# Five of eight row pairs of two matrix products by Strassen's algorithm, in an encoder kernel on one core

## The chip, the cores and the metric

The kernel runs on one core of one Trainium2 chip. The metric is the device time of one execution in microseconds; a lower time is better. The engines are TensorE (PE, with its weight loads PEld), VectorE (DVE), ScalarE (ACT), GpSimd (POOL) and SyncE (SP), which here only issues loads. SBUF is the memory that the engines compute from, PSUM the eight banks of 128 x 512 float32 that TensorE writes its sums to.

## What is computed

Two layers of an encoder on 256 tokens of width 2048, in float32. Cut to what matters:

```python
for l in range(DEPTH):                       # 2 layers
    u = rmsnorm(x, norm_mix[l])
    proj = u @ w_in[l]                       # 2048 x 8256: queries, keys, values, two gates
    ...                                      # y_a: latent attention @ w_o_mla, y_b: neighbourhood attention @ w_o_na
    merged = jax.nn.sigmoid(gate_a) * y_a + jax.nn.sigmoid(gate_b) * y_b
    x = x + merged @ w_out[l]                # 2048 x 2048
    h = rmsnorm(x, norm_mlp[l]) @ w_ff1[l]   # 2048 x 8192
    x = x + jnp.square(jax.nn.relu(h)) @ w_ff2[l]   # 8192 x 2048
return rmsnorm(x, norm_final)
```

## The kernel before

All products run on TensorE in a rounded float32 format. To keep float32 accuracy each operand is split in two: `hi`, the rounded value (a copy on ACT), and `lo`, the rest (a subtraction on DVE, `lo = raw - hi`, both inputs in SBUF). A product of two split operands takes three matmuls, hi x hi, hi x lo and lo x hi, summed in one PSUM bank.

Weights stream from memory through `weights` (L157): a load of 1 MB by SP into one of three `raw` buffers, ACT's cast to `hi` (L172) and DVE's subtraction to `lo` (L173), both on 128 x 1024 elements, into four `hi` and four `lo` buffers. There are two forms of product:

- `gemm_a` (L215) has the activations stationary (128 tokens by 128 rows) and 512 weight columns moving; its result has tokens on the partitions. It holds two banks, one per 128 tokens, and runs over 16 row blocks, two at a time: 96 matmuls for 512 columns. It serves w_out, w_ff2, the gates and the attention output products.
- `gemm_b` (L227) has the weights stationary and 256 tokens moving, hi and lo side by side in a 512-wide matmul, then a 256-wide one; its result is transposed, ready to be the next product's activation. It serves w_in's attention parts and w_ff1.

The MLP runs in four blocks of 2048 hidden columns. A block is four `gemm_b` of 512 hidden columns (w_ff1), whose results `relu2` (L639) adds up, squares and splits into `pair` tiles (hi and lo of 256 tokens), and four `gemm_a` (w_ff2), whose results `residual` (L612) adds to x (`xt`, L617 and L619), scaled there by the square of the row norm. In w_out, `turned` (L319) transposes the merged attention output on TensorE into the activations, column group by column group as the group is finished.

The order of the instructions comes from the program text and from a list scheduler at build time, which may move an instruction of an engine ahead of others; each engine then executes its own list strictly in order, with waits on the others. Small attention steps are slipped between matmuls by `tick`. PSUM is used as five banks under the tag `bank` and three under `abank` (`ABANKS`). POOL does little: the mask sum of the neighbourhood attention (L416), sums of squares (L275), a power of the norms (L259) and a few small loads.

Of the kernel before, what the change touches and what calls it, by code (L numbers as in the profile page):

```python
# [26 lines left out]
F32 = mybir.dt.float32  # L28
F32R = mybir.dt.float32r
# [26 lines left out]
NSLOT, ABANKS, SMALL, RBUFS, HBUFS = 44, 3, 8, 3, 4  # L56
# [6 lines left out]
def trunk(ctx: ExitStack, tc: tile.TileContext, x, w_in, w_uq, w_ukv, rpb, w_o_mla, w_o_na,  # L63
# [3 lines left out]
    wpool = ctx.enter_context(tc.tile_pool(name="wpool", bufs=4))  # L67
    slots = ctx.enter_context(tc.tile_pool(name="slots", bufs=NSLOT))
    tmp = ctx.enter_context(tc.tile_pool(name="tmp", bufs=2))
    psum = ctx.enter_context(tc.tile_pool(name="psum", bufs=8, space=bass.MemoryType.PSUM))  # L70

    def bank():
# [12 lines left out]
    def small():  # L85
        return tmp.tile([P, S], F32, tag="small", name="small", bufs=SMALL)
# [70 lines left out]
    def weights(w, nk, c0, n, before=None):  # L157
# [3 lines left out]
        for k0 in range(0, nk, 2):  # L161
# [6 lines left out]
            hi = wpool.tile([P, 1024], F32R, tag="hi", name="hi", bufs=HBUFS)  # L168
            lo = wpool.tile([P, 1024], F32R, tag="lo", name="lo", bufs=HBUFS)
# [6 lines left out]
    def weights_twice(w, nk, c0, n):  # L176
# [4 lines left out]
        for k0 in range(0, nk, 8):  # L181
            hi = wpool.tile([P, 1024], F32R, tag="hi", name="hi", bufs=HBUFS)
            lo = wpool.tile([P, 1024], F32R, tag="lo", name="lo", bufs=HBUFS)
# [58 lines left out]
    def rows_of(col):  # L242

        dg = [tmp.tile([P, P], F32, tag="diag", name="diag", bufs=4) for _ in range(2)]
# [6 lines left out]
        row = tmp.tile([P, S], F32, tag="rrow", name="rrow", bufs=4)  # L251
# [3 lines left out]
    def root(v, width, name):  # L255

        nc.vector.tensor_scalar(v, v, 1.0 / width, EPS, op0=ALU.mult, op1=ALU.add)  # L257
        col = tmp.tile([P, 2], F32, tag="rcol", name=name, bufs=6)
        nc.gpsimd.tensor_tensor(col, v, mhalf, op=ALU.pow)  # L259
        return col  # L260

    class Norm:
# [14 lines left out]
        def scales(self):  # L277
# [5 lines left out]
            v = tmp.tile([P, 2], F32, tag="var", name="var", bufs=2)  # L283
# [4 lines left out]
    class RowNorm:  # L288


        def __init__(self):
            self.sums = tmp.tile([P, 2, 4], F32, tag="sums", name="sums", bufs=2)

        def add(self, t, c4):
            junk = tmp.tile([P, 512], F32, tag="junk", name="junk", bufs=1)
# [3 lines left out]
        def scale(self):  # L299
            v = tmp.tile([P, 2], F32, tag="var", name="var", bufs=2)  # L300
# [3 lines left out]
        def scales(self):  # L304

            self.scale()
            self.half = tmp.tile([P, 2], F32, tag="rcol", name="half", bufs=6)
# [3 lines left out]
        def square(self):  # L311

            self.scale()
            self.sq = tmp.tile([P, 2], F32, tag="rcol", name="sq", bufs=6)
            nc.vector.tensor_tensor(self.sq, self.col, self.col, op=ALU.mult)
            return
            yield
# [157 lines left out]
    for l in range(DEPTH):  # L475
        wi = w_in[l]
# [116 lines left out]
        mg = [None] * NC  # L593
        for c4 in range(4):
            th = [None] * 2

            def merge(t, ps):
# [3 lines left out]
                if t == 1:  # L601
                    start(turned(lambda t, c4=c4: part[t, c4], c4, mg, lambda c: 0.5), 2)
# [4 lines left out]
            gemm_a(w_o_mla[l], c4 * 512, att, merge)  # L607


        last = l == DEPTH - 1  # L610

        def residual(c4, scale=None, n=None, then=None):  # L612

            def evac(t, ps):
                cs = xt[t][:, c4 * 512:(c4 + 1) * 512]
                if scale is None:
                    nc.vector.tensor_tensor(cs, cs, ps, op=ALU.add)  # L617
                else:
                    nc.vector.scalar_tensor_tensor(cs, ps, scale.sq[:, t:t + 1], cs, op0=ALU.mult, op1=ALU.add)  # L619
                if n is not None:  # L620
                    n.add(t, c4)
                if then is not None and t == 1:
                    start(then(c4), 2)
            return evac
# [3 lines left out]
        for c4 in range(4):  # L628
            gemm_a(w_out[l], c4 * 512, mg,
# [101 lines left out]
```

## Time and profile before

| | before |
|---|---|
| median of three runs, us | 2689.84 (2689.79 to 2690.21) |
| the profiled execution, us | 2689.91 |
| its span in the profile, us | 2688.1 |
| TensorE busy, us | 2666.8 (99%) |
| DVE busy, us | 1602.9 (60%) |
| ACT busy, us | 1277.1 (48%) |
| POOL busy, us | 60.5 (2%) |
| memory traffic, mean | 185 GB/s |

The span runs from the first to the last instruction that the profile records. A group of instructions is one line of the program on one engine with one shape; it has a count, its busy time, the mean duration of one in ns, and the idle time of its engine just before, with what ended that idle time. Matmuls overlap in the pipeline, so their durations add up to more than the time they take; the distance from one start to the next is what a matmul costs.

### The profile page before, as it was taken

What the parts mean: (1) busy time and instruction counts of PE and PEld (TensorE: products, weight loads), DVE (VectorE), ACT (ScalarE), POOL (GpSimd) and SP (SyncE); (2) the same over time, 40 slices, a digit from 0 to 9 for tenths busy, and PEclk for the clock granted to TensorE, in tenths of its full rate; (3) what the DMA queues carried; (4) which work ended last, traced back from release to release, by engine and by line L of the source; (5) the groups of instructions that cost most, each with busy time, mean ns of one, the idle gap of its engine ahead of it and who ended that gap; (6) DMA issues with size and microseconds to landing.
All of it is one profiled execution on the core that took longest, in us unless ns stands there. A gap on an engine that the chain in (4) does not pass through costs nothing.

```text
span 2688.1 us, 34037 instructions
## 1 busy us (share of the span) xinstructions
PE 2666.8 (99%) x13596; PEld 2268.7 (84%) x13596; DVE 1602.9 (60%) x2158; ACT 1277.1 (48%) x1815; POOL 60.5 (2%) x86
## 2 busy tenths in 40 slices
PE   8999999999999999999999999999999999999998
PEld 7888888888888888888888888888888888888886
DVE  5676486555655546556567754955556555565554
ACT  5554465444434434444445544644444344443443
POOL 1110000000000000000001100000000000000000
PEclk9999999999999999999999999999999999999999
DMA  7555644555565555555555555455555555655554
GB/s 231 184 165 189 195 161 155 189 184 180 186 203 186 190 190 186 197 193 189 183 183 179 171 187 183 153 167 188 188 188 188 189 187 194 208 189 193 188 188 141
DMA packets 253839, 496.49 MB, mean 185 GB/s; under 512 B 12688, under 2 KB 16784, under 8 KB 253680
## 3 DMA queue, kind: packets, MB, share of 16 engines
q1 hardware_dynamic: 250624, 488.14, 55.2%
q0 software_dynamic: 2048, 4.56, 0.6%
q8 instruction: 106, 1.74, 0.3%
q10 hardware_dynamic: 1008, 1.61, 0.2%
q14 instruction: 53, 0.43, 0.0%
HBM read 492.18 MB, written 2.10 MB: 184 GB/s over the span
## 4 chain that ended last, share of the span: by engine, by line
PE 84%; issue 14%; DVE 1%; DMA 1%; ACT 0%; POOL 0%; SPq 0%; POOLq 0%; DVEq 0%; ACTq 0%
PE bank L194 21%; PE bank L199 16%; PE bank L200 16%; PE bank L201 16%; PE bank L195 11%; DMA raw<-in_w_in 1%; PE abank L206 1%; PE abank L205 1%; PE abank L204 1%; PE abank L326 1%; PE abank L377 0%; DVE lo L173 0%; DVE wide L670 0%; PE abank L347 0%; ACT hi L172 0%
## 5 line engine op out<-in xcount | busy, mean ns | idle before, releaser
L173 DVE TENSOR_TENSOR lo<-raw,hi 128x1024 fp32r<-128x1024 f32 (+1 forms) x928 | 1132.5, 1222 | 977.8 <-ACT hi L172 973.0
L172 ACT CAST hi<-raw 128x1024 fp32r<-128x1024 f32 (+1 forms) x928 | 971.8, 1049 | 1131.1 <-PE bank L201 736.2
L194 PE MATMUL bank<-pair,hi 128*128 128x512 f32 x3008 | 1059.0, 398 | 2.3 <-DVE small L212 1.0
L200 PE MATMUL bank<-lo,pair 128*128 128x512 f32 (+1 forms) x2240 | 866.1, 387 | 0.0
L199 PE MATMUL bank<-hi,pair 128*128 128x512 f32 (+1 forms) x2240 | 865.8, 388 | 0.0
L201 PE MATMUL bank<-hi,pair 128*128 128x512 f32 (+1 forms) x2240 | 865.8, 387 | 0.0
L195 PE MATMUL bank<-pair,lo 128*128 128x256 f32 x3008 | 835.5, 280 | 0.4 <-DVE lo L173 0.3
L194 PEld LDWEIGHTS bank<-pair,hi 128*128 128x128 f32 x3008 | 563.5, 188 | 133.0 <-ACT hi L172 1.9
L195 PEld LDWEIGHTS bank<-pair,lo 128*128 128x128 f32 x3008 | 567.7, 189 | 5.9 <-DVE lo L173 1.6
L201 PEld LDWEIGHTS bank<-hi,pair 128*128 128x128 f32 x2240 | 420.8, 188 | 84.6
L199 PEld LDWEIGHTS bank<-hi,pair 128*128 128x128 f32 x2240 | 420.8, 188 | 84.1
L200 PEld LDWEIGHTS bank<-lo,pair 128*128 128x128 f32 x2240 | 420.9, 188 | 82.6
L150 ACT ACTIVATE pair<-small 128x256 fp32r<-128x256 f32 x200 | 73.6, 413 | 89.8 <-DVE small L641 67.1
L210 ACT COPY small<-bank 128x256 f32<-128x256 f32 x218 | 78.6, 369 | 29.0 <-PE bank L195 27.8
L152 DVE TENSOR_TENSOR pair<-small,pair 128x256 fp32r<-128x256 f32 x200 | 76.6, 418 | 19.2 <-ACT pair L150 19.2
L212 DVE TENSOR_TENSOR small<-bank,small 128x256 f32<-128x256 f32 x218 | 83.0, 416 | 0.2
L259 POOL TENSOR_TENSOR col<-var,mhalf 128x2 f32<-128x2 f32 x9 | 6.3, 702 | 1928.8 <-DVE var L257 1928.8
L619 DVE SCALAR_TENSOR_TENSOR xt<-bank,sq,xt 128x512 f32<-128x512 f32 x64 | 45.0, 744 | 7.8 <-PE bank L201 7.8
L641 DVE SCALAR_TENSOR_TENSOR small<-small 128x256 f32<-128x256 f32 x128 | 48.2, 418 | 0.0
L154 DVE SCALAR_TENSOR_TENSOR pair<-abank,g_sb,pair 128x256 fp32r<-128x256 f32 x64 | 29.2, 478 | 23.0 <-ACT pair L150 23.0
L150 ACT ACTIVATE pair<-abank,g_sb 128x256 fp32r<-128x256 f32 x64 | 28.2, 469 | 27.3 <-PE abank L326 23.4
L150 ACT ACTIVATE pair<-abank 128x256 fp32r<-128x256 f32 x64 | 23.6, 381 | 29.2 <-PE abank L206 19.1
(96 smaller groups left out, 789.9 us busy)
## 6 DMA issues: line engine op xcount, KB each, us to landing
raw<-in_w_ff SPq DMA_DIRECT2D x256, 1024.0 KB, 5.0
raw<-in_w_in SPq DMA_DIRECT2D x124, 1024.0 KB, 5.1
raw<-in_w_out SPq DMA_DIRECT2D x32, 1024.0 KB, 4.9
raw<-in_w_o_na SPq DMA_DIRECT2D x16, 1024.0 KB, 4.9
raw<-in_w_o_mla SPq DMA_DIRECT2D x16, 1024.0 KB, 4.9
raw<-in_w_ukv SPq DMA_DIRECT2D x8, 1024.0 KB, 4.9
raw<-in_w_uq SPq DMA_DIRECT2D x8, 768.0 KB, 4.6
raw<-in_w_in SPq DMA_DIRECT2D x10, 512.0 KB, 4.9
```

Source lines behind the costliest of these rows:

```text
L150: nc.scalar.activation(dst[:, :S], src, AF.Copy, scale=scale)
L152: nc.vector.tensor_tensor(dst[:, S:], src, dst[:, :S].bitcast(F32), op=ALU.subtract)
L172: nc.scalar.copy(hi, src)
L173: nc.vector.tensor_tensor(lo, src, hi.bitcast(F32), op=ALU.subtract)
L194: nc.tensor.matmul(ps, wh, a, start=first, stop=False)
L195: nc.tensor.matmul(ps[:, :S], wl, a[:, :S], start=False, stop=last)
L199: nc.tensor.matmul(ps, a[:, t * P:(t + 1) * P], wh, start=first, stop=False)
L200: nc.tensor.matmul(ps, a[:, t * P:(t + 1) * P], wl, start=False, stop=False)
L201: nc.tensor.matmul(ps, a[:, S + t * P:S + (t + 1) * P], wh, start=False, stop=last)
L210: nc.scalar.copy(h, ps[:, S:])
L212: nc.vector.tensor_tensor(t, ps[:, :S], h, op=ALU.add)
L641: nc.vector.scalar_tensor_tensor(t, t, 0.0, t, op0=ALU.max, op1=ALU.mult)
```

## The change

Rows of the weights are taken in pairs of 128 (`j`, eight pairs for 2048 rows), and columns in halves of 1024. For such a pair the product of a 2 x 2 block matrix of activations (two token halves by two row blocks) with a 2 x 2 block matrix of weights (two row blocks by two halves of 512 columns) needs eight block products, 24 matmuls. For the five pairs in `SPAIRS` the changed kernel forms it with seven block products (Winograd's form of Strassen's algorithm), 21 matmuls, from sums of blocks; the other three pairs run plainly and accumulate into the same banks. This is `gemm_s`, used for w_out and w_ff2; a call covers 1024 columns and holds all eight banks.

The sums of weight blocks are `t13` (POOL, 128 x 1024, two at once) and `t24` (its first half on POOL, its second on DVE). They, `b21` and the two diagonal blocks are split by ACT and DVE as the weights were. The sums of activation blocks (`s1` to `s4`) are made by POOL in `operand`, four instructions of 128 x 128, and split with the blocks. At the end `residual` makes the four output blocks from eight banks: eight DVE adds, one ACT copy and four POOL adds of 128 x 512.

```diff
-NSLOT, ABANKS, SMALL, RBUFS, HBUFS = 44, 3, 8, 3, 4
+NSLOT, SMALL, RBUFS, HBUFS = 44, 8, 3, 4
+
+SPAIRS = (0, 1, 3, 5, 7)
...
     def bank():
-        return psum.tile([P, 512], F32, tag="bank", name="bank", bufs=8 - ABANKS)
-
-    def abank():
-        return psum.tile([P, 512], F32, tag="abank", name="abank", bufs=ABANKS)
+        return psum.tile([P, 512], F32, tag="bank", name="bank", bufs=8)
+
+    abank = bank
...
+    def operand(f, strassen):
+        a11, a21, a12, a22, s1, s2, s3, s4 = (f[:, i] for i in range(8))
+        if strassen:
+            nc.gpsimd.tensor_tensor(s1, a21, a22, op=ALU.add)
+            nc.gpsimd.tensor_tensor(s2, s1, a11, op=ALU.subtract)
+            nc.gpsimd.tensor_tensor(s4, a12, s2, op=ALU.subtract)
+            nc.gpsimd.tensor_tensor(s3, a21, a11, op=ALU.subtract)
+        hi, lo = [], []
+        for i in range(0, 8 if strassen else 4, 4):
+            src = f[:, i:i + 4].rearrange("p a q -> p (a q)")
+            h, lw = pair(), pair()
+            nc.scalar.copy(h, src)
+            nc.vector.tensor_tensor(lw, src, h.bitcast(F32), op=ALU.subtract)
...
+    def turned_pair(src, c, dst, j):
+        tp = abank()
...
+        f = tmp.tile([P, 8, P], F32, tag="f", name="f", bufs=2)
+        nc.scalar.activation(f[:, :4].rearrange("p a q -> p (a q)"), tp, AF.Copy, scale=0.5)
+        dst[j] = operand(f, j in SPAIRS)
...
+    def gemm_s(w, c0, acts, evac):
...
+        for j in range(n):
+            raw = wpool.tile([P, 2048], F32, tag="raw", name="raw", bufs=RBUFS)
+            nc.sync.dma_start(raw.rearrange("p (k n) -> p k n", n=1024),
+                              w[2 * j * P:(2 * j + 2) * P, c0:c0 + 1024].rearrange("(k p) n -> p k n", p=P))
+            if j not in SPAIRS:
+                for k in range(2):
+                    left, right = half(raw[:, k * 1024:(k + 1) * 1024])
+                    ah, al = have(acts, j)
+                    for i, t, side in ((2, 0, right), (3, 0, left), (4, 1, right), (8, 1, left)):
+                        mm3(i, ah[2 * k + t], al[2 * k + t], *side)
...
+                continue
+            b12, b11, b22, b21 = (raw[:, i:i + 512] for i in range(0, 2048, 512))
+            t13 = wpool.tile([P, 1024], F32, tag="t", name="t13", bufs=4)
+            nc.gpsimd.tensor_tensor(t13.rearrange("p (a n) -> p a n", a=2),
+                                    b12.rearrange("p (a n) -> p a n", a=1).to_broadcast([P, 2, 512]),
+                                    raw[:, 512:1536].rearrange("p (a n) -> p a n", a=2), op=ALU.subtract)
+            t24 = wpool.tile([P, 1024], F32, tag="t", name="t24", bufs=4)
+            nc.gpsimd.tensor_tensor(t24[:, :512], b22, t13[:, :512], op=ALU.subtract)
+            nc.vector.tensor_tensor(t24[:, 512:], b21, t24[:, :512], op=ALU.subtract)
+            w11, w22 = half(raw[:, 512:1536])
+            w21, = half(b21)
+            w1, w3 = half(t13)
+            w2, w4 = half(t24)
+            (a11, _, a12, a22, s1, s2, s3, s4), low = have(acts, j)
+            (l11, _, l12, l22, r1, r2, r3, r4) = low
+            mm3(1, a11, l11, *w11)
+            mm3(2, a12, l12, *w21)
+            tick()
+            mm3(3, s4, r4, *w22)
+            mm3(5, s1, r1, *w1)
+            tick()
+            mm3(7, s3, r3, *w3)
+            mm3(6, s2, r2, *w2)
+            tick()
+            mm3(4, a22, l22, *w4)
+        evac(b)
...
+        half_a = ExitStack()
+        wpool = half_a.enter_context(tc.tile_pool(name="wpool", bufs=4, reuse_waits="tile"))
+        tmp = half_a.enter_context(tc.tile_pool(name="tmp", bufs=2, reuse_waits="tile"))
...
-                if t == 1:
-                    start(turned(lambda t, c4=c4: part[t, c4], c4, mg, lambda c: 0.5), 2)
...
+        drain()
+        half_a.close()
...
+        half_b = ExitStack()
+        hbufs, smalls = 5, 3
...
+        for c4 in range(4):
+            for c in range(2):
+                start(turned_pair(lambda t, c4=c4: part[t, c4], c, mg, 2 * c4 + c), 0)
...
+                nc.scalar.copy(p1, b[1])
+                nc.vector.tensor_tensor(x11, x11, b[2], op=ALU.add)
+                nc.gpsimd.tensor_tensor(x11, x11, p1, op=ALU.add)
+                nc.vector.tensor_tensor(x12, x12, b[3], op=ALU.add)
+                nc.vector.tensor_tensor(x22, x22, b[8], op=ALU.add)
+                nc.vector.tensor_tensor(x22, x22, b[5], op=ALU.add)
+                nc.vector.tensor_tensor(u2, p1, b[6], op=ALU.add)
+                nc.vector.tensor_tensor(u4, u2, b[5], op=ALU.add)
+                nc.vector.tensor_tensor(u3, u2, b[7], op=ALU.add)
+                nc.gpsimd.tensor_tensor(x12, x12, u4, op=ALU.add)
+                nc.vector.tensor_tensor(x21, x21, b[4], op=ALU.add)
+                nc.gpsimd.tensor_tensor(x22, x22, u3, op=ALU.add)
+                nc.gpsimd.tensor_tensor(x21, x21, u3, op=ALU.add)
```

The squared row norm is no longer multiplied in `residual`; instead `relu2` multiplies by the row norm before it squares. The weight and scratch pools (`wpool`, `tmp`) are opened anew for each half of a layer, one for the attention (four `hi` and `lo` buffers) and one for w_out and the MLP (five, and four `t` buffers).

How the scheduler places this is shown at three places. The first is DVE in a w_ff2 product. Before, in the first block of layer 0, behind the last `relu2`, splits of the weights alternate with the residual adds of a column group (`xt`, the two token halves):

```order
L641 SCALAR_TENSOR_TENSOR small<-small 128x256
L152 TENSOR_TENSOR pair<-small,pair 128x256
L173 TENSOR_TENSOR lo<-raw,hi 128x1024 x7
L619 SCALAR_TENSOR_TENSOR xt_91<-bank,sq,xt_91 128x512
L619 SCALAR_TENSOR_TENSOR xt_92<-bank,sq,xt_92 128x512
L173 TENSOR_TENSOR lo<-raw,hi 128x1024 x8
```

In the changed kernel, at the end of the first half of that product (`t13_6953` and `t24_6955` are the sums of the last pair, `t13_7014` and `t24_7016` those of the next half's first):

```order
L374 TENSOR_TENSOR lo_6963<-raw_6951,hi_6962 128x512
L374 TENSOR_TENSOR lo_6967<-t13_6953,hi_6966 128x1024
L397 TENSOR_TENSOR t24_7016<-raw_7012,t24_7016 128x512
L374 TENSOR_TENSOR lo_6971<-t24_6955,hi_6970 128x1024
L730 TENSOR_TENSOR xt1_89<-xt1_89,bank_6775 128x512
L727 TENSOR_TENSOR xt0_88<-xt0_88,bank_6692 128x512
L374 TENSOR_TENSOR lo_7020<-raw_7012,hi_7019 128x1024
L729 TENSOR_TENSOR xt0_88<-xt0_88,bank_6696 128x512
L374 TENSOR_TENSOR lo_7024<-raw_7012,hi_7023 128x512
L397 TENSOR_TENSOR t24_7067<-raw_7063,t24_7067 128x512
L731 TENSOR_TENSOR xt1_89<-xt1_89,bank_6700 128x512
L374 TENSOR_TENSOR lo_7028<-t13_7014,hi_7027 128x1024
```

The splits of the next half's first pair stand between the residual adds of the half that ends, and each pair has five DVE instructions in place of two.

The second place is POOL over the same stretch. Before, its list goes from the norms of the attention (L275 sums, L259 powers) straight to the loads of the next layer's attention bias:

```order
L259 TENSOR_TENSOR col<-var,mhalf 128x2
L275 TENSOR_TENSOR acc<-acc,small 128x256 x3
L259 TENSOR_TENSOR col<-var,mhalf 128x2 x3
L412 DMA mb<-in_rpb 64x6x64 x4
L416 TENSOR_TENSOR mb<-mb,mask_sb 128x384 x2
```

In the changed kernel, from the last hidden pair of the block on:

```order
L326 TENSOR_TENSOR f_6640<-f_6640 128x128
L392 TENSOR_TENSOR t13_6875<-raw_6873 128x1024
L396 TENSOR_TENSOR t24_6877<-raw_6873,t13_6875 128x512
L392 TENSOR_TENSOR t13_6953<-raw_6951 128x1024
L396 TENSOR_TENSOR t24_6955<-raw_6951,t13_6953 128x512
L392 TENSOR_TENSOR t13_7014<-raw_7012 128x1024
L396 TENSOR_TENSOR t24_7016<-raw_7012,t13_7014 128x512
L392 TENSOR_TENSOR t13_7065<-raw_7063 128x1024
L396 TENSOR_TENSOR t24_7067<-raw_7063,t13_7065 128x512
L728 TENSOR_TENSOR xt0_88<-xt0_88,u_6995 128x512
L392 TENSOR_TENSOR t13_7144<-raw_7142 128x1024
```

POOL now has two subtractions for each Strassen pair, and its residual adds stand in the same list.

The third place is DVE at the end of a block's w_ff1. Before, the results of the last column group (L212 add, L641 square, L152 split) come between the splits of two weight loads of w_ff2:

```order
L212 TENSOR_TENSOR small<-bank,small 128x256 x3
L641 SCALAR_TENSOR_TENSOR small<-small 128x256 x3
L173 TENSOR_TENSOR lo<-raw,hi 128x1024
L212 TENSOR_TENSOR small<-bank,small 128x256
L152 TENSOR_TENSOR pair<-small,pair 128x256 x3
```

In the changed kernel `small` and `rrow` (the row norm) belong to the last four `relu2`, the `lo` and `t24` to the first two pairs of w_ff2:

```order
L374 TENSOR_TENSOR lo_6673<-raw_6665,hi_6672 128x1024
L397 TENSOR_TENSOR t24_6720<-raw_6716,t24_6720 128x512
L374 TENSOR_TENSOR lo_6677<-raw_6665,hi_6676 128x512
L374 TENSOR_TENSOR lo_6681<-t13_6667,hi_6680 128x1024
L374 TENSOR_TENSOR lo_6685<-t24_6669,hi_6684 128x1024
L770 TENSOR_TENSOR small_6626<-bank_6451,small_6624 128x256
L771 SCALAR_TENSOR_TENSOR small_6626<-small_6626,rrow_5971 128x256
```

All splits of the first pair (`raw_6665`) and the subtraction of the second (`t24_6720`) stand ahead of the last `relu2`, which is where w_ff1's last matmuls end.

More of the change, by code (lines that the diff above doesn't have):

```diff
@@ L242, in rows_of @@
     def rows_of(col):
-        dg = [tmp.tile([P, P], F32, tag="diag", name="diag", bufs=4) for _ in range(2)]
+        dg = [keep.tile([P, P], F32, tag="diag", name="diag", bufs=4) for _ in range(2)]
         for t in range(2):
@@ L627, in trunk, with scaled_mlp @@
         xg = [None] * NC
-        for c4 in range(4):
-            gemm_a(w_out[l], c4 * 512, mg,
-                   residual(c4, None, mlp, lambda c4, xg=xg: turned_x(c4, xg, G_MLP + l * NC)))
-        start(mlp.square(), 10)
+        for g in range(2):
+            gemm_s(w_out[l], g * 1024, mg,
+                   residual(g, mlp, lambda c4, xg=xg: turned_x(c4, xg, G_MLP + l * NC)))
+        def scaled_mlp():
+            start(mlp.scales(), 0)
+            while not hasattr(mlp, "row"):
+                advance(len(pending) - 1)
         norm = RowNorm()
```

130 lines of the change are left out of this document (84 added, 46 removed).

## The prediction

> **What bounds it now.** I read the page's busy shares and chain first, then the stretch in which the change sits, then its groups, and last the few places where POOL computes.
>
> ```profile
> span 2688.1 us, 34037 instructions
> PE 2666.8 (99%) x13596; PEld 2268.7 (84%) x13596; DVE 1602.9 (60%) x2158; ACT 1277.1 (48%) x1815; POOL 60.5 (2%) x86
> PE 84%; issue 14%; DVE 1%; DMA 1%; ACT 0%; POOL 0%; SPq 0%; POOLq 0%; DVEq 0%; ACTq 0%
> ```
>
> TensorE is busy in 2666.8 of 2688.1 us and carries the chain; 21 us are all that other engines cost it. The profiled execution took 2689.91 us, 1.8 beyond its span and within 0.1 of the median 2689.84. I add to 2689.9. A difference under 0.2% (5 us) I count as no change.
>
> The next fence has the busy time by stretch for one w_ff2 product of a block and the w_ff1 products behind it (columns: us, then PE, PEld, DVE, ACT, POOL busy and count, granted clock, DMA share, GB/s).
>
> ```profile
> 729.20:816.30 87.10, 87.10 (x386) 72.18 (x385) 46.98 (x50) 35.29 (x38) 0.00 (x0) 1.00 0.57 191
> 816.30:905.90 89.60, 89.60 (x513) 78.00 (x512) 52.57 (x72) 42.56 (x60) 0.00 (x0) 1.00 0.57 189
> ```
>
> The first stretch is four column groups of 96 matmuls. TensorE has no gap, so one matmul of 512 columns costs 87.10/384 = 0.2268 us. POOL does nothing there, and DVE is idle for nearly half.
>
> **What is removed.** A pair of row blocks takes 24 matmuls plainly and 21 by Strassen. There are 20 products of 1024 columns (2 layers, 1 in w_out and 4 in w_ff2, 2 halves), each with five such pairs: 20 x 5 x 3 = 300 matmuls, 300 x 0.2268 = 68.0 us. One product of 1024 columns goes from 192 x 0.2268 = 43.5 to 177 x 0.2268 = 40.1 us of TensorE; a Strassen pair is 4.76 us of it.
>
> **What is added: operands for DVE and POOL.** A plain pair needs two splits of 1024. A Strassen pair needs three of 1024, one of 512 and a subtraction of 512 on DVE, and subtractions of 1024 (t13) and 512 (t24) on POOL. The groups that price them:
>
> ```profile
> L173 DVE TENSOR_TENSOR lo<-raw,hi 128x1024 fp32r<-128x1024 f32 x32 | 39.2, 1225 | 39.6 <-ACT hi L172 39.4
> L172 ACT CAST hi<-raw 128x1024 fp32r<-128x1024 f32 x33 | 34.8, 1055 | 50.0 <-PE bank L201 49.7 <-PE bank L194 0.2
> L188 DVE TENSOR_TENSOR lo<-raw,hi 128x512 fp32r<-128x512 f32 x8 | 5.2, 689 | 5.3 <-ACT hi L187 5.3
> L187 ACT CAST hi<-raw 128x512 fp32r<-128x512 f32 x8 | 4.6, 618 | 7.8 <-PE bank L194 7.8
> L617 DVE TENSOR_TENSOR xt<-xt,bank 128x512 f32<-128x512 f32 x16 | 10.2, 681 | 0.0
> L641 DVE SCALAR_TENSOR_TENSOR small<-small 128x256 f32<-128x256 f32 x128 | 48.2, 418 | 0.0
> L379 ACT CAST pp<-abank 128x512 fp32r<-128x512 f32 x32 | 18.7, 584 | 17.3 <-PE abank L377 17.1
> ```
>
> DVE per Strassen pair: 3 x 1.225 + 2 x 0.689 = 5.05 us; per plain pair 2.45. ACT per Strassen pair: 3 x 1.055 + 0.618 = 3.8, under TensorE's 4.76, so ACT costs nothing. DVE per product of 1024: 5 x 5.05 + 3 x 2.45 + 8 residual adds of 0.681 = 38.1 us, just under TensorE's 40.1. Were POOL independent, TensorE would stay the bound. Whether it is independent is seen where it computes beside DVE (timeline: start, us, engine and line).
>
> ```profile
> 103.65 1.01 POOL L416 TENSOR_TENSOR mb<-mb,mask_sb 128x384 f32<-128x384 f32 x1 [3.61 <-DMA mb<-in_rpb]
> 192.74 0.74 POOL L275 TENSOR_TENSOR acc<-acc,small 128x256 f32<-128x256 f32 x1 [1.66 <-ACT small L274]
> 108.28 1.01 POOL L416 TENSOR_TENSOR mb<-mb,mask_sb 128x384 f32<-128x384 f32 x1 [2.13 <-DMA mb<-in_rpb]
> 108.46 1.91 DVE L173 TENSOR_TENSOR lo<-raw,hi 128x1024 fp32r<-128x1024 f32 x1
> 182.49 1.22 DVE L173 TENSOR_TENSOR lo<-raw,hi 128x1024 fp32r<-128x1024 f32 x1 [0.42 <-ACT hi L172]
> 182.82 1.76 POOL L416 TENSOR_TENSOR mb<-mb,mask_sb 128x384 f32<-128x384 f32 x1 [2.62 <-DMA mb<-in_rpb]
> 189.91 1.16 POOL L275 TENSOR_TENSOR acc<-acc,small 128x256 f32<-128x256 f32 x1 [5.33 <-ACT small L274]
> 190.39 0.42 DVE L212 TENSOR_TENSOR small<-bank,small 128x256 f32<-128x256 f32 x1
> 214.31 1.23 DVE L173 TENSOR_TENSOR lo<-raw,hi 128x1024 fp32r<-128x1024 f32 x1 [0.22 <-ACT hi L172]
> 215.46 1.36 DVE L154 SCALAR_TENSOR_TENSOR pair<-small,g_sb,pair 128x256 fp32r<-128x256 f32 x2
> ```
>
> At 108.28 POOL runs to 109.29; the split that starts inside it takes 1.91 instead of 1.225, as if begun at 109.14, 0.15 before POOL's end. At 182.49 it is the other way round: POOL takes 1.76 instead of 1.01, as if begun 0.14 before the split's end. So a split (two SBUF inputs) and a POOL instruction exclude each other, with 0.15 us of overlap at a handover. DVE at 190.39, with one input in PSUM, keeps its 0.42 inside a POOL instruction: the residual adds are not excluded. (The Trainium skill, SBUF — State Buffer, section Who interferes with whom, states the exclusion for every VectorE instruction with two SBUF inputs against a GpSimd instruction that reads SBUF; the trace agrees with 1.91 for 1.225, and by that rule the subtractions and operand splits, whose forms no row here shows, are excluded too.)
>
> POOL's clean 0.74 for 256 and 1.01 for 384 elements make 2.11 ns an element and 0.20 us fixed: an estimate of 2.36 us for 1024, 1.28 for 512, 0.47 for 128, reaching 2.7 times beyond the longest row. (The Trainium skill, GPSIMD Engine Reference, section Elementwise — side-by-side cycle accounting, gives 4497 ns for 2048 elements; by its half and quarter, an estimate, the sum below would be some 45 us smaller. The trace's slope is kept.)
>
> Exclusive time of a Strassen pair: 5.05 + 2.36 + 1.28 = 8.69; less four handovers of 0.15, and 0.07 for each of three DVE instructions that follow another DVE instruction (214.31 + 1.23 is 215.54, the next starts at 215.46): 7.9 us, against TensorE's 4.76. Ends: 8.69 without any overlap, 7.5 if every instruction costs only its row less 0.15 and POOL's fixed part vanishes at its borders.
>
> **Sum for one w_ff2 block (two products of 1024 columns), from the last w_ff1 matmul on.** Ten Strassen pairs 79.0; six plain ones 14.7; POOL's four residual adds of the first half 4 x 1.28 = 5.1; the last hidden pairs still to be formed 5.7 (four POOL of 0.47, three DVE of 0.689, four of 0.418). Ready ahead, as the order shows: the first pair 7.9 and the second's POOL part with its DVE subtraction 4.3, so -12.2. The last product after its split: 1.0. The eight DVE residual adds run under POOL's instructions: 0, with 5.4 per product as the other end. Total 93.3 us, against 87.1: +6.2. Behind it w_ff1 waits 1.5 for its first split, queued behind two residual adds of 0.681 (the next five are made while TensorE works on three). Eight blocks: 8 x 7.7 = +62.
>
> **w_out.** Nothing is ready ahead here: the transposed operands start only after the first half's pools close. Added to 79.0 + 14.7 + 5.1 + 1.0: 20 POOL instructions of 0.47 and 13 DVE splits of 0.689 for the operands, 18.4; and a start during which TensorE waits for bank copy 0.584, four POOL 1.9, cast 0.618, cast of the weights 1.055 and a first split, about 5 (0 if the order hides it, 7 with all handovers). 123.2 against 87.1 (the same 384 matmuls before), and 1.5 behind: +37.6, twice +75.
>
> ```profile
> raw<-in_w_ff SPq DMA_DIRECT2D x256, 1024.0 KB, 5.0
> SPq L167 <- DVE lo L173: 1909.6, 369, 9.1
> ```
>
> **Smaller edits.** Loads keep their number and size and wait for buffers (second row), not for the DMA; one per 4.76 us is the fastest demand, with three buffers for 5.0 us of landing: 0. Between the layers the pools change once more, with a load and a split to wait for, and the last residual chain (DVE adds, two POOL adds of 1.28, norm) is longer: 5 each, +10. The per-row scale that moves from the residual to relu2 replaces an operand of an existing instruction: 0, hidden in w_ff1, where DVE is busy for 52.57 of 89.60. One tag for all eight banks: 0, since a half's banks are freed while its last products run; if not, 0.7 per half.
>
> Sum: 62 + 75 + 10 = +147, in which the 68 us of removed matmuls are contained. 2689.9 + 147 = 2837 us.
>
> **Rivals.**
> 1. *POOL is hidden, faster.* POOL's instructions fall where DVE waits for ACT's casts (39.6 us in the stretch above), and TensorE stays the bound: -68 + 2 x 5 + 10 x 1.5 + 10 = -33, 2657 us. For it: DVE alone needs 38.1 of 40.1. Against it: in those waits DVE has no split ready, but the splits then only come later, and exclusive time is 93 in 87. It decides where a Strassen pair's exclusive time is under 7.05 us (with H for it, a block with its wait behind is 9 H + 23.7 by the sum above, and 87.1 at 7.05); full gain below 6.3.
> 2. *Residual not covered.* DVE's order puts residual adds that wait for the last products ahead of the next splits; all 5.4 us per product then count: 20 x 5.4 = +108, 2945 us. For it: DVE executes in order. Against it: most splits of the next pair stand between the adds.
> 3. *The clock falls.* TensorE waits 7.9 - 4.76 = 3.1 us in each of three Strassen pairs in a row (last of one half, first two of the next). At half clock these 14.3 us double, of which the waits absorb 9: +5 to +14 per block, ten blocks, 2887 to 2977.
>
> ```profile
> 0.00:18.00 18.00, 9.71 (x32) 7.16 (x32) 2.59 (x4) 7.43 (x15) 7.34 (x18) 1.00 0.88 258
> ```
>
>    Against it: TensorE busy for only 9.71 of these 18 us, and the granted clock stays 1.00. (The Trainium skill, TensorE: Matmul & The Clock Gate, section Part 1: The HAM clock gate, halves the clock after an idle window of about 3.4 us; by that rule waits of 3.1 would just escape. This row shows no fall.)
>
> **Chances.** My sum 0.58, with its own range 2750 to 2940 (100 Strassen pairs x -0.4, four more instructions ready ahead per block -36 and no start -10, to x +0.8 and a quarter of rival 2's adds); rival 2 0.13; rival 3 0.04; rival 1 0.20; the sum meeting its point of balance, no change, 0.03; 0.02 for a slight gain or loss of other cause. Faster 0.22, same 0.03, slower 0.75. For 8 in 10 the range runs from 2675, inside rival 1, to 2960.
>
> **What would show it.** Right: TensorE busy for about 92% of the span (2666.8 - 68 in 2835) with waits on lo splits in the w_out and w_ff2 stretches; the 1024 splits' mean well over 1225 ns, and POOL's t13 well over 2.36 where they meet; DVE and POOL busy times together near the length of those stretches. Matmuls of 512 columns 300 fewer at 0.2268 either way. Wrong: split means still at 1225 with POOL active, TensorE without gaps in w_ff2, or the POOL instruction of 1024 far from 2.36.

## The result, and the profile after

The changed kernel takes 2912.32 us (median of four runs, 2906.73 to 2917.03), the kernel before 2689.82 (2688.95 to 2690.21) on the same chip. The ratio is 1.0827, 95% interval 1.0807 to 1.0847: slower, by 222.5 us. The forecast was 2837 with a range of 2675 to 2960.

The first two parts of the page after (busy time of each engine; then the span in 40 slices, with the granted clock):

```profile
PE 2715.9 (93%) x13304; PEld 2241.7 (77%) x13304; DVE 2204.2 (76%) x2514; ACT 1499.9 (52%) x2149; POOL 839.6 (29%) x566
...
PE   8999999879989899899889999998899898998996
...
POOL 1110000362352543534401100003524435435244
PEclk9999999899999999999899999999999999999998
```

TensorE is busy for longer than before (2666.8) with 300 fewer matmuls of 512 columns (292 fewer in all; in part because some of them run at half clock, see the last section), and its row shows gaps where POOL's row shows work: the stretches with w_out and the MLP. What TensorE waits for (us in all, times, longest), and then the groups of DVE and POOL in those stretches with different shapes kept apart:

```profile
PE bank L368 <- DVE lo L374: 123.4, 106, 3.8
PE bank L368 <- ACT hi L373: 11.4, 8, 4.8
PE bank L368 <- DVE small L770: 11.0, 8, 1.8
```

```profile
L374 DVE TENSOR_TENSOR lo<-raw,hi 128x1024 fp32r<-128x1024 f32 x220 | 376.0, 1737 | 10.6 <-ACT hi L373 10.0
L374 DVE TENSOR_TENSOR lo<-t,hi 128x1024 fp32r<-128x1024 f32 x200 | 281.4, 1422 | 8.2 <-ACT hi L373 7.8
L333 DVE TENSOR_TENSOR pair<-f,pair 128x512 fp32r<-128x512 f32 x130 | 127.3, 983 | 15.1 <-ACT pair L332 14.8
L397 DVE TENSOR_TENSOR t<-raw,t 128x512 f32<-128x512 f32 x100 | 112.2, 1122 | 90.4 <-POOL t L396 90.4
```

```profile
L392 POOL TENSOR_TENSOR t<-raw x100: 2357/2593/3527, 553.3 to 2882.0; 128x1024 f32<-128x1024 f32 x100
```

Before, TensorE waited 7.4 us for the input and at most 1.0 for any other cause; now 123.4 us for `lo`, and once in each block 1.3 to 1.8 for an add of `relu2` (`small`) that stands in DVE's order behind L397, which itself waits there some 4 us for POOL's `t`. The same 128 x 1024 split took 1225 ns and takes 1737 in the mean. `t13` (L392: shortest, median, longest) takes 2357 ns where nothing disturbs it, the estimate of 2.36, and half of them take 2593 or more. Why they stretch is seen where two of them meet (DVE first, then POOL):

```profile
998.25 2.85 DVE L397 TENSOR_TENSOR t<-raw,t 128x512 f32<-128x512 f32 x1 [4.17 <-POOL t L396]
1001.03 2.28 DVE L374 TENSOR_TENSOR lo<-raw,hi 128x1024 fp32r<-128x1024 f32 x1
```

```profile
998.18 2.38 POOL L392 TENSOR_TENSOR t<-raw 128x1024 f32<-128x1024 f32 x1
1000.63 1.59 POOL L396 TENSOR_TENSOR t<-raw,t 128x512 f32<-128x512 f32 x1
```

DVE's subtraction starts inside POOL's `t13` and ends at 1001.10, 0.54 after POOL's end: it did its 0.68 from 0.14 before that end on. POOL's next instruction starts inside it and ends at 1002.22; DVE's next split, 1.22 by itself, ends 1.09 later. One of the two always waits, and nothing of it is idle time in any row: it shows as longer instructions.

Where the time went, by the start of the first `max` of `relu2` in a block (L641 before, L771 after; us, in the traces; a steady block is half the way from the second block's to the fourth's):

| | first block, layer 0 | steady block, layer 0 | first block, layer 1 | span |
|---|---|---|---|---|
| before | 661.8 | 176.7 | 1992.6 | 2688.1 |
| after | 706.5 (+44.7) | 190.3 (+13.6) | 2155.4 | 2911.7 |

Two w_outs make 89, eight blocks 109, and some 25 are left for the change of layers and the end. A steady block, first its w_ff1, then the stretch from the last w_ff1 matmul to DVE's last residual adds:

```profile
876.00:962.00 86.00, 86.00 (x490) 74.70 (x489) 67.60 (x73) 45.88 (x67) 27.98 (x23) 1.00 0.59 196
962.00:1066.30 104.30, 91.47 (x379) 71.26 (x378) 92.01 (x85) 54.57 (x65) 48.82 (x25) 0.97 0.46 161
```

(length; busy time of PE, PEld, DVE, ACT, POOL; granted clock.) w_ff1 keeps TensorE without a gap. In w_ff2 DVE and POOL are busy for 92.0 and 48.8 of 104.3 us, more than the stretch together, since each counts its waiting for the other as busy. From w_ff1's last matmul to the next w_ff1's first (962.46 to 1062.55, 100.1 us; 87.1 before) one of the two is busy for 97.8 us: as one line they leave almost nothing free.

### The profile page after: what moved, and what is told of

It reads as the page before. It is cut to its first block, busy times and chain, and to the rows that moved or that the text cites. A ratio compares the mean times of both kernels' runs of the same rounds, so it can differ in the third digit from the quotient of the medians.

```text
span 2911.7 us, 34973 instructions
## 1 busy us (share of the span) xinstructions
PE 2715.9 (93%) x13304; PEld 2241.7 (77%) x13304; DVE 2204.2 (76%) x2514; ACT 1499.9 (52%) x2149; POOL 839.6 (29%) x566
## 3 DMA queue, kind: packets, MB, share of 16 engines
q0 software_dynamic: 2048, 4.56, 0.6%
## 4 chain that ended last, share of the span: by engine, by line
PE 45%; DVE 15%; DMA 6%; POOL 6%; issue 5%; ACT 2%; POOLq 0%; DVEq 0%; SPq 0%; ACTq 0%
PE bank L202 16%; DVE lo L374 10%; PE bank L368 9%; PE bank L203 8%; DMA raw<-in_w_ff 6%; PE bank L207 4%; PE bank L209 4%; PE bank L208 4%; POOL t L392 3%; POOL t L396 2%; DVE t L397 1%; DVE lo L181 1%; DVE pair L333 1%; ACT hi L373 1%; ACT hi L180 0%
## 5 line engine op out<-in xcount | busy, mean ns | idle before, releaser
L181 DVE TENSOR_TENSOR lo<-raw,hi 128x1024 fp32r<-128x1024 f32 (+1 forms) x608 | 765.7, 1267 | 492.3 <-ACT hi L180 491.2
L180 ACT CAST hi<-raw 128x1024 fp32r<-128x1024 f32 (+1 forms) x608 | 631.3, 1044 | 666.7 <-PE bank L209 304.3
L368 PE MATMUL bank<-hi,pair 128*128 128x512 f32 x2360 | 775.3, 409 | 27.4 <-ACT hi L373 11.4
L368 PE MATMUL bank<-lo,pair 128*128 128x512 f32 x1180 | 493.4, 421 | 123.8 <-DVE lo L374 123.4
L374 DVE TENSOR_TENSOR lo<-raw,hi 128x1024 fp32r<-128x1024 f32 x320 | 470.8, 1507 | 17.6 <-ACT hi L373 17.0
L392 POOL TENSOR_TENSOR t<-raw 128x1024 f32<-128x1024 f32 x100 | 271.0, 2710 | 543.2 <-DMA raw<-in_w_ff 473.9
L207 PE MATMUL bank<-hi,pair 128*128 128x512 f32 (+1 forms) x960 | 370.8, 387 | 0.0
L373 ACT CAST hi<-raw 128x1024 fp32r<-128x1024 f32 x320 | 281.7, 913 | 170.0 <-PE bank L368 161.4
L209 PE MATMUL bank<-hi,pair 128*128 128x512 f32 (+1 forms) x960 | 369.2, 385 | 0.0
L208 PE MATMUL bank<-lo,pair 128*128 128x512 f32 (+1 forms) x960 | 366.6, 382 | 0.0
L374 DVE TENSOR_TENSOR lo<-t,hi 128x1024 fp32r<-128x1024 f32 x200 | 281.4, 1422 | 8.2 <-ACT hi L373 7.8
```

What stands on the lines that cost most here:

```text
L180: nc.scalar.copy(hi, src)
L181: nc.vector.tensor_tensor(lo, src, hi.bitcast(F32), op=ALU.subtract)
L207: nc.tensor.matmul(ps, a[:, t * P:(t + 1) * P], wh, start=first, stop=False)
L208: nc.tensor.matmul(ps, a[:, t * P:(t + 1) * P], wl, start=False, stop=False)
L209: nc.tensor.matmul(ps, a[:, S + t * P:S + (t + 1) * P], wh, start=False, stop=last)
L368: nc.tensor.matmul(b[i], x, y, start=count[i] == 1, stop=count[i] == total[i])
```

## Experiments

Theory A: DVE and POOL exclude each other, and their time one after the other sets the pace. Rival B: the loads come late because raw buffers are held. Rival C: TensorE loses its clock in the waits. All ratios are to the kernel before, in runs on the same chip.

**The weight subtractions on VectorE.** L392 and L396:

```
-            nc.gpsimd.tensor_tensor(t13.rearrange("p (a n) -> p a n", a=2),
+            nc.vector.tensor_tensor(t13.rearrange("p (a n) -> p a n", a=2),
...
-            nc.gpsimd.tensor_tensor(t24[:, :512], b22, t13[:, :512], op=ALU.subtract)
+            nc.vector.tensor_tensor(t24[:, :512], b22, t13[:, :512], op=ALU.subtract)
```

> t13 and the first half of t24 are made by DVE in place of POOL; the sums are the same. DVE's work per Strassen pair grows from 5.05 to 6.96 us (3 x 1.225 + 0.689 + 1.225 + 2 x 0.689), 190 us more in all for 100 pairs. Theory A (a POOL instruction and a DVE instruction with two SBUF inputs exclude each other): the 3.64 us of POOL were paid by DVE anyway, so the time stays about where it is, 2830 to 2930 us. Rival B (the cost is the loads: a raw buffer is held until DVE has split it, and POOL then waits for the next load): DVE is slower per pair and holds the buffers longer, 3000 to 3100 us. If engines were independent and DVE merely full: 3050 or more.

2844.56 us, 1.0578 [1.0547, 1.0609]: 68 us faster than the change, with 199 us of instructions moved onto the engine that TensorE waits for. DVE:

```profile
L374 DVE TENSOR_TENSOR lo<-raw,hi 128x1024 fp32r<-128x1024 f32 x220 | 274.4, 1266 | 2.4 <-ACT hi L373 2.0
L374 DVE TENSOR_TENSOR lo<-t,hi 128x1024 fp32r<-128x1024 f32 x200 | 260.1, 1304 | 23.7 <-ACT hi L373 23.4
L392 DVE TENSOR_TENSOR t<-raw 128x1024 f32<-128x1024 f32 x100 | 130.5, 1305 | 61.0 <-DMA raw<-in_w_ff 54.6 <-DMA raw<-in_w_out 6.4
```

DVE is busy for 2143.1 us in all, 61 less than in the change. `t13` takes 1.3 us there for POOL's 2.4 at the least. This is A's range; by B it would have been 3000 or more.

**No subtractions.** L391 to L397 removed; the four combined blocks are split straight from `raw`.

```
-            w1, w3 = half(t13)
-            w2, w4 = half(t24)
+            w1, w3 = half(raw[:, 0:1024])
+            w2, w4 = half(raw[:, 1024:2048])
```

> t13 and t24 are not computed at all; their splits read the raw weights again, so ACT's and DVE's splits and all matmuls are as many as before and the output is not the reference's. Left out per Strassen pair: 3.64 us of POOL and 0.689 of DVE. Theory A: exclusive time per pair falls from 7.9 to 4.1 us, under TensorE's 4.76; w_ff2 becomes bound by TensorE (80 us a block for 100 now), w_out loses about 30 us a layer: 2680 to 2740 us. Rival B (loads held by the splits): the raw buffers now wait for four splits instead of two and the subtractions, so little is gained: 2850 or more.

2727.82 us, 1.0144 [1.0107, 1.0181]. The subtractions, with what they do to the splits, are 184 of the 222 us; a steady block is down to 174.7, 2.0 under the block before. With 300 matmuls fewer it is still 38 us slower than before (the interval lies above 1): what is left is in w_out (first `relu2` at 680.4, +18.6) and at the change of layers.

**GpSimd fills instead of subtracting.** The same two POOL instructions write a constant and read nothing.

```
-            nc.gpsimd.tensor_tensor(t13.rearrange("p (a n) -> p a n", a=2),
...
+            nc.gpsimd.memset(t13, 0.5)
-            nc.gpsimd.tensor_tensor(t24[:, :512], b22, t13[:, :512], op=ALU.subtract)
+            nc.gpsimd.memset(t24[:, :512], 0.5)
```

> POOL's two subtractions per Strassen pair are replaced by two fills of the same tiles with a constant (t13 1024 wide, t24 512 wide), which read nothing from SBUF; DVE's subtraction and all splits stay, the output is not the reference's. Theory A in the form that only POOL's reads exclude DVE: the splits go back to a mean of 1.23 us and the time to 2690 to 2750 us. A in the form that any POOL instruction excludes DVE: splits stay over 1.3 us and the time is 2760 to 2850, by the length of the fills. Rival B: t13 no longer waits for the load, so 2750 to 2850 too, but with splits that need not change.

2769.25 us, 1.0298 [1.0268, 1.0328]. By its total this lies in the range of "any POOL instruction excludes DVE" (2760 to 2850) and in B's, and 19 us above that of "only POOL's reads exclude". The durations say otherwise: the splits of `raw` are back at 1229 ns (1737 in the change), those of `t` at 1317 (1422).

```profile
L374 DVE TENSOR_TENSOR lo<-raw,hi 128x1024 fp32r<-128x1024 f32 x220 | 262.8, 1229 | 10.7 <-ACT hi L373 9.7
```

And single rows settle it (POOL, then DVE):

```profile
964.23 0.96 POOL L392 MEMSET t<- 128x1024 f32 x1 [9.10 <-DVE lo L374]
...
973.48 0.96 POOL L392 MEMSET t<- 128x1024 f32 x1 [2.34 <-DVE lo L374]
```

```profile
962.96 2.35 DVE L374 TENSOR_TENSOR lo<-t,hi 128x1024 fp32r<-128x1024 f32 x2
...
973.94 1.21 DVE L374 TENSOR_TENSOR lo<-t,hi 128x1024 fp32r<-128x1024 f32 x1
```

The splits that lie over a fill keep their 1.21 (two in a row 2.35), and the fills their 0.96. It is POOL's reading that excludes. (The Trainium skill, SBUF — State Buffer, section Who interferes with whom, says so: two SBUF inputs on VectorE against a GpSimd instruction that reads SBUF, not one that only writes. These rows agree.) What lies above the first range was not taken apart; DVE's own subtraction stayed in this run, and POOL's other instructions that read.

**Four raw buffers.** One more raw buffer in the second part of a layer; its room came from one u tile, one rrow, two diag tiles and the DMA scratch.

```
-            raw = wpool.tile([P, 2048], F32, tag="raw", name="raw", bufs=RBUFS)
+            raw = wpool.tile([P, 2048], F32, tag="raw", name="raw", bufs=rbufs)
...
-        hbufs, smalls = 5, 3
+        hbufs, smalls, rbufs = 5, 3, 4
```

> Four raw buffers in place of three in the half with w_out and the MLP (room is made by three u, three rrow and two diag buffers and a smaller DMA scratch). Theory A: POOL and DVE are the bound, the loads only follow; 2885 to 2915 us. Rival B: POOL's waits for loads before t13 (474 us in the profile) shrink to less than a third, and the time falls by 60 us or more, to 2780 to 2850.

2917.31 us, 1.0848 [1.0817, 1.088]: no gain. POOL waits for loads before `t13` for 338 us instead of 474, and TensorE waits 108 us for `lo` instead of 123, but now also 27 for residual adds. To see whether the missing u tile causes these, the run was done again with all u tiles (the room from one slot instead).

> The change with four raw buffers in the second part of a layer, and all four u tiles kept (the room is taken from one slot, one rrow, two diag tiles and the DMA scratch; in the first kernel with four raw buffers a u tile was missing, and TensorE waited 26 us for residual adds that it did not wait for in the change). Open are some 38 of the 75 us by which the change exceeds the prediction; VectorE stands still for 90 us before L397, for a t that GpSimd makes after a wait for a load. If the late loads are that rest: 2860 to 2890. If a buffer more only makes VectorE wait inside its splits instead: 2900 to 2920.

2914.06, 1.0835 [1.0803, 1.0866]. TensorE waits 27 us for residual adds here too, so the u tile was not their cause. B falls as far as one more buffer can show it: the buffer only moves the place of the wait.

**The clock.** Three of a pair's seven products get a fourth matmul, so that TensorE has less to wait.

```
-            for x, y in ((ah, wh), (ah, wl), (al, wh)):
+            for x, y in ((ah, wh), (ah, wl), (al, wh)) + (((al, wh),) if again and i in (1, 5, 6) else ()):
```

> Three of the seven products of a Strassen pair get a fourth matmul (the third again, on the same tiles), so the sums differ: 300 more matmuls, as many as the kernel before has, 68 us of TensorE at 0.2268 us. The subtractions and loads are the change's own. Theory A with C (VectorE and GpSimd set the pace, and part of the loss is matmuls at half clock after waits): the extra work falls into TensorE's waits (123 us for the splits) and keeps it busy, the time at half clock falls from 133 us to under 90, and the time comes out at 2850 to 2925, at best below the changed kernel's 2912 though there is more to compute. A without C (half clock only fills time in which TensorE would wait anyway): 2905 to 2945. If TensorE's own work set the time: 2912 + 68 = 2980.

2934.44 us, 1.0911 [1.089, 1.0933]: 22 us more for 68 us of added TensorE work, with the granted clock up from 0.975 to 0.982 (133 us at half clock before the end of the change, 92 here). Two thirds of the work vanish in the waits, so TensorE is not the bound; and a better clock did not pay for the rest, which speaks against C. No run changes the clock alone.

**Three pairs for five.** `SPAIRS = (0, 1, 5)`.

> Three Strassen pairs (0, 1 and 5) of eight in place of five, all else as the change. Theory A: a half of 1024 columns has 3 x 7.9 + 5 x 2.5 = 36.2 us of VectorE and GpSimd one after the other for 41.5 us of TensorE, so TensorE is the bound again in most of it and the loss is no longer in step with the number of pairs: 2700 to 2790. If each Strassen pair costs a fixed amount: 2690 + 222 x 3 / 5 = 2823, 2800 to 2850.

2796.62 us, 1.0399 [1.0378, 1.042], between the two ranges. The steady block tells more: 178.7, that is 2.0 above the block before for three pairs and 13.6 for five. The cost grows far faster than the number of pairs, as A has it once the two engines' time exceeds TensorE's; four pairs were not run, so where it sets in is not shown. The total just missed A's range: w_out still costs 32 us a layer (first `relu2` at 694.2), and the change of layers some 26.

**Without VectorE's residual adds.** To see where the forecast fell short:

```
-                nc.vector.tensor_tensor(x11, x11, b[2], op=ALU.add)
...
+                nc.scalar.copy(u2, b[6])
+                nc.scalar.copy(u4, b[5])
+                nc.scalar.copy(u3, b[7])
```

> The change without VectorE's eight residual adds of 128 x 512 per product of 1024 columns (three banks are copied by ScalarE instead, four are not read); GpSimd's four adds stay, so the output lacks these sums. The prediction costed the eight at nothing, since they have an input in PSUM and run under GpSimd's instructions; the trace of the change shows most of them with GpSimd idle. If they cost nothing: 2900 to 2915. If all count, as in the second rival: 2912 - 20 x 5.4 = 2804, 2790 to 2830. Half: 2850 to 2870.

2875.37 us, 1.0691 [1.0671, 1.071]: 37 us less, net of the three copies that ScalarE makes instead; a third of the 108 that they would cost if nothing covered them. In the change's trace 91 of the 160 adds run with POOL idle throughout, and only 40 of their 109 us lie under a POOL instruction. One in the middle of a block (DVE, then POOL, which is idle from 1015.46 on, then TensorE):

```profile
1015.93 0.67 DVE L731 TENSOR_TENSOR xt<-xt,bank 128x512 f32<-128x512 f32 x1
1016.53 1.21 DVE L374 TENSOR_TENSOR lo<-t,hi 128x1024 fp32r<-128x1024 f32 x1
```

```profile
1018.52 3.21 POOL L392 TENSOR_TENSOR t<-raw 128x1024 f32<-128x1024 f32 x1 [3.06 <-DMA raw<-in_w_ff]
```

```profile
1017.80 0.79 PE L368 MATMUL bank<-lo,pair 128*128 128x512 f32 x1 [3.16 <-DVE lo L374]
```

The add stands ahead of the split that TensorE waits for, and nothing covers it.

Both together, no adds and four raw buffers:

> The same without VectorE's eight residual adds per product, as in the run without adds (2875), so the output lacks these sums. If loads and adds are two separate causes: 2825 to 2850, about the 2837 that was predicted. If more buffers bring nothing: 2860 to 2885.

2874.95, 1.0689 [1.0658, 1.072]: the buffer adds nothing here either. This pair also bears on C: the two spans are 2873.3 and 2872.0 at mean clocks of 0.974 and 0.984, so some 57 us less at half clock (2 x 0.010 x 2872) went with a difference of 1. The two also differ in the buffer, so this is a sign and not a proof.

**A version that keeps DVE below TensorE.** w_out plainly as before; two Strassen pairs, all subtractions on DVE; the banks that end with the last Strassen pair are added up two plain pairs later, on DVE.

```
-SPAIRS = (0, 1, 3, 5, 7)
+SPAIRS = (0, 3)
...
+                if j == SPAIRS[-1] + 2:
+                    evac(b, True)
```

> w_out plainly as before; in the second MLP product two Strassen pairs (0 and 3) of eight, all their subtractions on VectorE, and the sums of the banks that end with the last Strassen pair are added up two plain pairs later, on VectorE, so that only four adds stand at the end of a half. Saved: 3 matmuls x 2 pairs x 16 halves = 96, 21.8 us. Theory A (nothing of GpSimd beside the splits, VectorE some 37 us a half against 42 of TensorE): 2665 to 2695. Rival (the eight banks held through a half, and the reordered first MLP product, cost by themselves): 2700 to 2740.

2716.28 us, 1.01 [1.0085, 1.0116]: the rival's range, and 21 us above A's. And three pairs, `SPAIRS = (0, 2, 4)`:

> As the two-pair kernel with three Strassen pairs (0, 2 and 4): 144 matmuls fewer than before, 32.7 us. VectorE has 3 x 7.1 + 5 x 2.5 + 7 = 41 us a half against 41.5 us of TensorE, so A gives between no further gain and a small loss: 2660 to 2710. If VectorE has room: 11 us below the two-pair kernel. Rival (a cost of the banks or of each pair): 2710 to 2760.

2705.59, 1.0059 [1.0043, 1.0076], inside A's range. The third pair brings 10.7 us where its matmuls are 10.9: DVE had the room. So both carry the same 48 us of something else. TensorE's waits in the three-pair kernel show part of it:

```profile
PE bank L202 <- ACT hi L180: 12.1, 3, 4.2
...
PE bank L258 <- DVE diag L254: 5.9, 1, 5.9
```

Two of the three waits for a first cast, 3.9 each at 649 and 1992, stand at the start of w_ff1 behind the change of pools in each layer, where no weight was loaded and cast ahead; the wait for the norm's diag, 5.9, is at the change of layers. Hence the last version, with the pools opened once; `u` and `f` share the buffers of `th`, `t` has two, and the norm's scales start six ticks after w_out.

```
-        drain()
-        half_a.close()
+        start(mlp.scales(), 6)
...
-            while pending:
-                drain()
-        half_b.close()
```

> The three-pair kernel without its change of pools in the middle and at the end of a layer (u and f tiles take the buffers of th, t has two buffers, the norm's scales start among the first products' ticks). The two- and three-pair kernels lie 48 and 48.5 us above 2689.8 less their removed matmuls, whatever the pairs; the trace shows 6 us of it at the drain behind w_out and 6 at the first loads behind it, in each layer, and as much between the layers. If the change of pools is that loss: 2675 to 2690, under the kernel before. If the loss is of the banks held or of the reordered first product: 2695 to 2706.

2684.88 us (eleven runs, 2684.36 to 2685.32), 0.9982 [0.9973, 0.9991]: 227 us faster than the change, and 4.6 below the kernel before, clear of the noise but under the 5 us that the prediction counts as no change. The first line of its page, and DVE's splits of `t` in w_ff2:

```profile
PE 2654.7 (99%) x13460; PEld 2246.0 (84%) x13460; DVE 1871.5 (70%) x2492; ACT 1400.1 (52%) x2015; POOL 160.6 (6%) x182
```

```profile
L364 DVE TENSOR_TENSOR lo<-t,hi 128x1024 fp32r<-128x1024 f32 x96 | 117.5, 1225 | 55.4 <-ACT hi L363 55.4
```

TensorE is at 99% again and the splits at 1225 ns. Of the 32.7 us of removed matmuls 28 are still lost: a steady block is 174.6, 2.1 below the block before where the matmuls are 4.1, and the first `relu2` comes at 668.3, 6.5 late. What makes these two was not tried.

## Why the prediction was right in sign and mechanism, and low in size

- *TensorE bounds, 300 matmuls of 0.2268 go.* Right for the kernel before; in the change it is busy 93% of the span (forecast 92%) and waits on `lo`, as the prediction's last part named.
- *Exclusion of DVE and POOL, 0.15 us of overlap, POOL's price 2.36 and 1.28 us.* Right, though taken from rows of 384 elements at most for POOL: 2357 ns is the shortest `t13`, 1.29 an undisturbed L396 (at 996.93). The runs with the subtractions moved, removed and replaced by fills show the mechanism itself.
- *The trace's slope against half the figure of the Trainium skill (GPSIMD Engine Reference, section Elementwise — side-by-side cycle accounting).* The trace's was the right one to keep: half of 4497 ns is 2.25 us, measured are 2.36 at the least. With its fixed part the trace's slope gives 4.52 us for 2048 elements, so it is the halving that misleads, and not the figure.
- *w_out: +37.6 each.* Measured +44.7 up to the first `relu2`, the start of 5 us as said (TensorE waits 4.78 there). Without the residual adds it is +38.5: the term lacked these.
- *w_ff2 block: +7.7.* The main error: measured +13.6, 47 us over eight blocks. The step that failed is "The eight DVE residual adds run under POOL's instructions: 0". They are not excluded by POOL (those under a POOL instruction keep their 0.68), as the prediction had it, but POOL is mostly idle when they come, so they lengthen DVE's own line. Taken out, a block falls to 187.5 (+10.8) and a w_out to +38.5; two and eight of them make 35 of the 37 us. The term was 0 with 5.4 per product as its other end (rival 2); it measured 1.9 per product, 37 over 20.
- *"Behind it w_ff1 waits 1.5 for its first split".* This did not come: w_ff1's first matmul starts one matmul's distance behind w_ff2's last.

```profile
1062.33 0.39 PE L368 MATMUL bank<-hi,pair 128*128 128x512 f32 x1
1062.55 0.63 PE L202 MATMUL bank<-pair,hi 128*128 128x512 f32 x2
```

  The 12 us that it put into the sum over eight blocks made the total better by luck.
- *What remains of a block.* In the block from 962.46 on, w_ff2's stretch is 13.0 longer than before where +6.2 was forecast, and w_ff1 takes 90.4 for 89.7. The adds are 2.8 of it; some 4 in w_ff2, 0.4 a Strassen pair, lie within the prediction's own range for the pair (7.9 -0.4 to +0.8). Which of its parts it is stays open; a fourth raw buffer did not recover it.
- *Loads 0.* Right: four buffers changed nothing, twice.
- *Changes of pools and layers: +10.* Low: some 25 us are left for it in the change. Opening the pools once, with the earlier scales and other buffers, saved 21 us in the version with three pairs (changes in the middle and at the end of a layer); the parts were not run one by one.
- *Rival 1, POOL hidden.* Its point of balance, 7.05 us of exclusive time a pair, was not reached by five pairs; with three the block comes within 2.0 us of the block before.
- *Rival 3, the clock.* What failed is the argument against it, and with it "by that rule waits of 3.1 would just escape". The row of the first 18 us shows a granted clock of 1.00, but its matmuls run at half speed: one of 512 columns takes 0.43 us to the next start (14.40 to 14.83), and 0.25 after it (20.25 to 20.50). The trace has no record of the clock before 18.2 us, and the view then shows 1.00. (The kernel before:)

```profile
14.40 0.63 PE L194 MATMUL bank<-pair,hi 128*128 128x512 f32 x1
14.83 0.63 PE L195 MATMUL bank<-pair,lo 128*128 128x256 f32 x2
...
20.25 0.40 PE L194 MATMUL bank<-pair,hi 128*128 128x512 f32 x1
20.50 0.28 PE L195 MATMUL bank<-pair,lo 128*128 128x256 f32 x1
```

  In the change the clock does fall, 27 times before the end, 133 us in all, and to 0.975 in the mean. The rival's price of 5 to 14 us a block is not seen: of the two runs without residual adds the one with 57 us less at half clock took the same time.

## What to carry to other kernels

An engine that helps can cost more than it takes over: where POOL reads SBUF while DVE has both inputs there, the two work one after the other, and work moved from POOL to DVE, which did it in about half the time (1.3 for 2.4 us), made the kernel faster. Before trading matmuls for additions, add up the additions, splits and residual adds on that one line for each product and compare with TensorE's time for the same product; with five pairs of eight the kernel lost 8%; with three, kept on DVE and in one of the two products alone, it broke even. An instruction is hidden only under work that runs beside it in the order, not under the sum of another engine's work.

## What the chip showed that was not expected

The granted clock changes in steps of 3.41 us (every stretch at half clock before the end of this trace is one, two, three or four of them), and a step need not be idle to bring it down. After the wait before the first of these matmuls TensorE worked again for the last sixth of the step, and still got half the clock in the next, in which it had no gap (windows of the change, one step each; PE's busy time is the second number, the clock the third from the end):

```profile
1003.36 0.50 PE L368 MATMUL bank<-lo,pair 128*128 128x512 f32 x1 [3.63 <-DVE lo L374]
...
1004.38 0.63 PE L368 MATMUL bank<-hi,pair 128*128 128x512 f32 x1
1004.80 0.63 PE L368 MATMUL bank<-lo,pair 128*128 128x512 f32 x1
```

```profile
1000.49:1003.90 3.41, 0.54 (x2) 0.49 (x3) 3.41 (x3) 1.04 (x1) 1.66 (x2) 1.00 0.00 0
1003.90:1007.31 3.41, 3.41 (x9) 2.64 (x8) 3.41 (x5) 0.56 (x1) 0.00 (x0) 0.50 0.72 231
```

```profile
570.41:573.82 3.41, 1.62 (x6) 0.67 (x4) 3.41 (x2) 1.80 (x2) 3.18 (x2) 1.00 0.77 288
573.82:577.24 3.42, 2.97 (x7) 2.42 (x8) 3.42 (x4) 2.68 (x4) 2.32 (x2) 0.50 0.02 8
587.48:590.89 3.41, 1.69 (x7) 1.07 (x7) 3.41 (x3) 1.17 (x2) 3.41 (x4) 1.00 0.12 48
590.89:594.30 3.41, 3.41 (x19) 2.77 (x18) 3.41 (x4) 1.06 (x1) 3.33 (x3) 1.00 0.02 5
```

1.62 us of work in a step of 3.41 were followed by half clock, 1.69 were not. Of the 27 falls in this trace 26 come behind a step in which TensorE was busy for under half, one behind 0.62 of a step; past the start no step at full clock with less than 0.46 was without a fall. Between 0.46 and 0.50 it went either way. (Some records of matmuls can be missing from a trace, so these shares are close and not exact.) (The Trainium skill, TensorE: Matmul & The Clock Gate, section Part 1: The HAM clock gate, has the same step of 3.4 us but an idle window as the condition; here a half-empty one sufficed.) At half clock a matmul of 512 columns comes every 0.43 us (from 1004.38 to 1004.80), instead of every 0.2268.

The other is how little that seems to have cost: in the two runs without residual adds, 57 us more or less at half clock went with the same time, in kernels in which TensorE waits some 100 us for DVE.
